# Expert blocks with a split down product, ScalarE evictions and g_ffn applied to the sums

## The chip, the cores and the metric

The kernel runs on 1 core of one Trainium2 chip, as a single launch. The metric is the device time of that core in microseconds (us). Before the change it is 3193.36 us, the median of 3 runs (3192.7 to 3193.63).

## The reference, cut to what matters

The whole is two transformer blocks on 512 tokens of width 1024 in float32. The change is in the expert layer of the first block, and in what follows it at once:

```python
def moe_ffn(h, ...):                      # n = 512 tokens, 64 experts, 8 chosen for each token
    scores = sigmoid(h @ w_router)
    idx = top_k(scores + b_router, 8)
    wts = scores[idx] / sum(scores[idx]) * 2.5
    # each expert works on its own tokens, in blocks of 128 places
    for tok, wt, e in blocks:
        yb = (silu(h[tok] @ w_gate[e]) * (h[tok] @ w_up[e])) @ w_down[e] * wt[:, None]
        routed = routed.at[tok].add(yb)
    return swiglu(h, w_sh_gate, w_sh_up, w_sh_down) + routed

x = x + g_ffn * moe_ffn(h2, ...)          # then a root mean square norm, then the second block
```

An expert has w_gate and w_up of 1024x256 and w_down of 256x1024. On average it has 512 x 8 / 64 = 64 tokens, so of the 128 places of a block about half are empty.

## The kernel before, in words

The engines are TensorE (PE), VectorE (DVE), ScalarE (ACT), GpSimd (POOL) and SyncE (SP). Every engine works through its own list of instructions in the order in which it is written. A scheduling pass of the compiler sets this order ahead of time, for the most part; in a few stretches, such as the end of the last expert, the order of some engines is written out by hand.

Most products are made in float32r, a faster form of float32 that rounds its operands. To keep precision an operand is split (`split`, lines 104 to 106): ScalarE copies it to float32r, the high half `hi` (L105), and VectorE subtracts that from the source, the low half `lo` (L106). `mm` (L102) then makes three passes: hi with hi, hi with lo, lo with hi. The halves of weights are called whi and wlo, 128x1024 each; they come from the pool `pair`, which has three buffers of each name and hands them out in turn. A product that isn't split is made in float32 itself; TensorE then works it off in two pieces.

The expert stage (`moe`) goes through 64 experts and one spare block, 65 blocks, each by `expert_block` (lines 1039 to 1077):
- GpSimd gathers the block's rows of h (`next_rows`, three buffers xg), skipping empty places. TensorE turns them in eight transposes (L1046, p_xt); the result is split into xt, hi and lo.
- The weights come from SyncE's queue as three tiles raw of 1 MB, gate and up in the first two, down in the third; nine such buffers rotate. Gate and up are split in four steps of 1024 columns; each step feeds six products into p_gu (L102), 24 in all.
- ScalarE takes the Silu of the gate part (L1060), VectorE multiplies by the up part (L1061, ea), TensorE turns ea in two transposes (L1064, p_at), VectorE copies the result to eat (L1066).
- The down product (L1072) is float32: eat with the raw weights, four products of 512 columns in eight pieces, into two banks p_y.
- VectorE evicts p_y and multiplies by the routing weight of the place and by the row g_ffn, `grow` (L1075, ey). GpSimd scatters ey and adds it to the rows of a DRAM buffer (L1076). There are two such buffers `yd` and they take turns; empty places go to 128 spare rows below the 512 real ones.

Between the blocks stand other pieces of work: the shared expert (`shared`, `shared_down`), tables of places for the next eight experts (`slots`), the turning of x (`by_tokens`). At the end `routed_first` and `routed_second` read the first buffer yd and add it to the residual rows; a loop for further blocks follows, with no turn when there are none; and `routed` (lines 1200 to 1228) reads the second buffer, adds it, and starts the norm.

Of the kernel before, what the change touches and what calls it, by code (L numbers as in the profile page):

```python
# [10 lines left out]
F32 = mybir.dt.float32  # L11
# [44 lines left out]
class K:  # L56
# [133 lines left out]
    def block1(self):  # L190
        nc, A = self.nc, self.A
        with ExitStack() as es:
# [4 lines left out]

            self.yd = [d.tile([640, 1024], F32, name=f"yd{i}") for i in range(2)]
            self.dr = d = self.pool(es, "b1_dram", space=DRAM)
# [90 lines left out]
    def qkv(self, q, s, w, ctx, mod, hc):  # L290
# [22 lines left out]
        for g in range(7):  # L313
            if g:
                w = self.load_pair(A["w_qkv"][g])
            for j in range(2):
# [25 lines left out]
                elif t < 10:  # L342
                    if t == 8:

                        nc.vector.tensor_copy(self.macc[:, 0:1], d[:, 0:1])
                        nc.vector.memset(self.macc, 0.0)
                        for y in self.yd:
                            for i in range(5):
                                nc.gpsimd.dma_start(y[128 * i:128 * i + 128, :], self.macc)
# [357 lines left out]
    def ffn_begin(self, q):  # L707
# [7 lines left out]
        self.lb = r.tile([128, 64], F32, name="lb")  # L715
        self.r4 = r.tile([128, 4], F32, name="r4")
        r = self.pool(self.rs, "h2r", side="right")
        rows = r.tile([128, 4, 1024], F32, name="h2rows")
# [45 lines left out]
    def moe(self):  # L764
        nc, tc, A = self.nc, self.tc, self.A
        with ExitStack() as es:
# [4 lines left out]
            self.sact = q.tile([128, 2, 512], F32, name="sact")  # L771
            self.grow = q.tile([128, 1024], F32, name="grow")
            self.xr = [t.rearrange("p a b -> p (a b)").rearrange("p (t d) -> p t d", d=1024) for t in self.h2f]
# [265 lines left out]
    def expert_block(self, xg, gi, ws, w, yd):  # L1039
# [20 lines left out]
        nc.scalar.activation(a, pg[:, :256], AF.Silu)  # L1060
        nc.vector.tensor_mul(a, a, pg[:, 256:])  # L1061
        pt = ps.tile([128, 512], F32, name="p_at", tag="tb")
        for k in range(2):
            nc.tensor.transpose(pt[:, 128 * k:128 * k + 128], a[:, 128 * k:128 * k + 128], self.ident)  # L1064
        at = ms.tile([128, 256], F32, name="eat", tag="eat")
        nc.vector.tensor_copy(at, pt[:, :256])  # L1066
        y = ms.tile([128, 1024], F32, name="ey", tag="ey")
        wd = part(2)
        for n in range(2):
            py = ps.tile([128, 512], F32, name="p_y", tag="y")  # L1070
            for k in range(2):
                nc.tensor.matmul(py, at[:, 128 * k:128 * k + 128], wd[:, 1024 * k + 512 * n:1024 * k + 512 * n + 512],  # L1072
                                 start=k == 0, stop=k == 1)
            o = slice(512 * n, 512 * n + 512)
            nc.vector.scalar_tensor_tensor(y[:, o], py, ws, self.grow[:, o], ALU.mult, ALU.mult)  # L1075
        nc.gpsimd.indirect_dma_start(out=yd[:], out_offset=bass.IndirectOffsetOnAxis(ap=gi, axis=0),  # L1076
                                     in_=y[:], in_offset=None, bounds_check=639, oob_is_err=True, compute_op=ALU.add)

# [65 lines left out]
    def routed_second(self):  # L1144
        for x, y in zip(self.xr, self.y0):
            self.nc.vector.tensor_add(x, x, y)

# [52 lines left out]
    def routed(self, q):  # L1200
# [14 lines left out]

        for t in range(4):
            nc.vector.tensor_add(x[t], x[t], ys[t])
            nc.vector.tensor_mul(self.v[:, t, :], x[t], self.gf)
            nc.scalar.activation(junk, x[t], AF.Square, accum_out=s[:, t, 0:1])

            nc.vector.tensor_scalar(s[:, t, 2:3], s[:, t, 0:1], EPS / 1024, EPS * EPS, op0=ALU.mult, op1=ALU.add)
            nc.scalar.activation(junk, self.v[:, t, :], AF.Square, accum_out=s[:, t, 1:2])
            nc.scalar.activation(s[:, t, 3:4], s[:, t, 1:2], AF.Sqrt, bias=s[:, t, 2:3], scale=1.0 / 1024)
            if t:
                scaled(t - 1)
# [1038 lines left out]
```

## Time and profile before

| what | value |
|---|---|
| median of 3 runs | 3193.36 us |
| the profiled execution | 3194.67 us, its span 3192.8 us |
| busy: TensorE, VectorE, ScalarE, GpSimd | 3071.1, 2237.8, 1384.8, 584.6 us |
| expert stage | from about 626 to 1364 us of the span |
| granted TensorE clock, mean | 0.986 |

The span runs from the first to the last instruction; the profiled execution's own time is 1.9 us longer. Busy times are means over stages that have different limits, so the stage that the change touches is read by itself: its windows, what waits in it for what, and the order in time of a few blocks. The end of a matmul in the trace is modelled and products overlap, so the pitch between starts tells what a product takes, not the length shown. A count such as x2 means that rows next to each other were merged. Several instructions of VectorE or ScalarE in a row overlap by a little too.

### The profile page before, as it was taken

How to read it: one execution, taken by the hardware profiler on the slowest of the kernel's cores; microseconds unless marked ns; L12 is line 12 of the kernel's file. 1: busy time of each engine (PE TensorE's matmuls, PEld its weight loads, DVE VectorE, ACT ScalarE, POOL GpSimd, SP SyncE). 2: the span in 40 equal slices, each digit the busy share in tenths (PEclk: the TensorE clock that was granted, in tenths of full speed). 3: DMA queues.
4: the chain of work that ended last, by engine and by line, in shares of the span. 5: the costliest groups of instructions: out<-in, count | busy, mean ns of one | idle time of the engine just before them, and what ended most of it. 6: DMA issues, size and time to landing. Idle time of an engine off the chain costs nothing.

```text
span 3192.8 us, 45059 instructions
## 1 busy us (share of the span) xinstructions
PE 3071.1 (96%) x16976; PEld 2576.9 (81%) x16976; DVE 2237.8 (70%) x4077; ACT 1384.8 (43%) x2195; POOL 584.6 (18%) x452
## 2 busy tenths in 40 slices
PE   7989999999999999969999999999999999999997
PEld 4777888666666766657778788899899999999997
DVE  6567644587777777757633234899998878888885
ACT  5357422454444544434444324444444443333332
POOL 0200000122222222200000000033333322222221
PEclk9999999899999999989999999999999999999999
DMA  7554545399999999952121123387799999999996
GB/s 243 177 155 146 204 172 187 127 356 339 337 342 333 358 354 346 305 172 80 56 72 68 60 93 131 123 295 273 266 329 357 329 333 336 345 344 341 350 342 194
DMA packets 236494, 779.99 MB, mean 244 GB/s; under 512 B 28772, under 2 KB 108132, under 8 KB 190452
## 3 DMA queue, kind: packets, MB, share of 16 engines
q1 hardware_dynamic: 167136, 570.88, 48.7%
q0 software_dynamic: 66368, 200.38, 20.6%
q10 hardware_dynamic: 2772, 5.85, 0.6%
q8 instruction: 134, 2.20, 0.3%
q14 instruction: 84, 0.69, 0.1%
HBM read 692.29 MB, written 101.97 MB: 249 GB/s over the span
## 4 chain that ended last, share of the span: by engine, by line
PE 46%; DVE 5%; issue 4%; ACT 1%; DMA 1%; POOL 0%; POOLq 0%; ACTq 0%; DVEq 0%
PE p_y L102 17%; PE p_pu L102 11%; PE p_za L102 3%; PE p_z L102 2%; PE p_all L1267 1%; PE p_rg L102 1%; PE p_yr L102 1%; PE p_mx L102 1%; DVE wlo L106 1%; DVE prow L2002 1%; PE r_s L1614 1%; PE r_y L1624 1%; PE p_ya L102 1%; PE p_gt L1971 1%; PE p_gt L1972 1%
## 5 line engine op out<-in xcount | busy, mean ns | idle before, releaser
L105 ACT ACTIVATE whi<-raw 128x1024 fp32r<-128x1024 f32 (+1 forms) x686 | 711.4, 1048 | 1115.5 <-PE p_pu L102 261.3
L106 DVE TENSOR_TENSOR wlo<-raw,whi 128x1024 fp32r<-128x1024 f32 (+1 forms) x686 | 822.0, 1206 | 370.4 <-ACT whi L105 361.1
L102 PE MATMUL p_pu<-xp,whi 128*128 128x384 f32 x2048 | 531.9, 338 | 5.0 <-ACT pact L1837 4.8
L102 PEld LDWEIGHTS p_pu<-xp,whi 128*128 128x128 f32 x2048 | 369.4, 188 | 8.0 <-ACT pact L1837 7.6
L102 PE MATMUL p_gu<-whi,xt 128*128 128x512 f32 x1040 | 357.1, 411 | 0.3 <-ACT whi L105 0.2
L102 PE MATMUL p_pu<-xp,wlo 128*128 128x384 f32 x1024 | 344.7, 338 | 4.5 <-DVE wlo L106 4.2
L102 PE MATMUL p_y<-vhi,wlo 128*128 128x384 f32 x1024 | 342.0, 334 | 0.0
L102 PE MATMUL p_y<-vlo,whi 128*128 128x384 f32 x1024 | 342.0, 334 | 0.0
L102 PE MATMUL p_y<-vhi,whi 128*128 128x384 f32 x1024 | 288.8, 334 | 1.4 <-ACT pkept L1837 1.4
L1992 POOL DMA_INDIRECT prow<-in_pu_rows,rows x128 | 197.6, 1544 | 405.4 <-DVE prow L2002 365.4
L1072 PE MATMUL p_y<-raw,eat 128*128 128x512 f32 x520 | 236.2, 595 | 2.7 <-DVE eat L1066 1.5
L102 PEld LDWEIGHTS p_gu<-whi,xt 128*128 128x128 f32 x1040 | 197.6, 191 | 50.6 <-issue 11.0
L102 PE MATMUL p_gu<-wlo,xt 128*128 128x512 f32 x520 | 223.0, 429 | 4.9 <-DVE wlo L106 4.7
L1992 POOL DMA_INDIRECT prow<-in_pv_rows,rows x128 | 140.6, 1099 | 369.3 <-DVE yr L2008 356.1
L102 PEld LDWEIGHTS p_pu<-xp,wlo 128*128 128x128 f32 x1024 | 192.3, 188 | 10.0 <-DVE wlo L106 9.6
L102 PEld LDWEIGHTS p_y<-vlo,whi 128*128 128x128 f32 x1024 | 192.3, 188 | 0.0
L102 PEld LDWEIGHTS p_y<-vhi,wlo 128*128 128x128 f32 x1024 | 192.2, 188 | 0.0
L102 PEld LDWEIGHTS p_y<-vhi,whi 128*128 128x128 f32 x1024 | 187.5, 188 | 1.7 <-ACT pkept L1837 1.7
L1072 PEld LDWEIGHTS p_y<-raw,eat 128*128 128x128 f32 x520 | 97.4, 191 | 101.6 <-issue 89.7
L1076 POOL DMA_INDIRECT yd<-ey,gidx x64 | 117.5, 1836 | 283.7 <-DVE ey L1075 266.5
L2008 DVE SCALAR_TENSOR_TENSOR yr<-prow,pdots,yr 128x1024 f32<-128x1024 f32 x128 | 163.7, 1279 | 0.2
L2002 DVE SCALAR_TENSOR_TENSOR prow<-prow,xr 128x1024 f32<-128x1024 f32 x128 | 155.3, 1216 | 1.8 <-DMA prow<-in_pu_rows,rows 1.7
(704 smaller groups left out, 5550.8 us busy)
## 6 DMA issues: line engine op xcount, KB each, us to landing
raw<-in_w_moe SPq DMA_DIRECT2D x195, 1024.0 KB, 12.2
raw<-in_pu SPq DMA_DIRECT2D x64, 1024.0 KB, 6.6
raw<-in_pv_rows SPq DMA_DIRECT2D x64, 1024.0 KB, 8.1
raw<-in_w_mod SPq DMA_DIRECT2D x24, 1024.0 KB, 6.1
gd<-gst SPq DMA_DIRECT2D x12, 2048.0 KB, 13.5
vgt<-gd SPq DMA_DIRECT2D x32, 768.0 KB, 11.4
actd<-pact SPq DMA_DIRECT2D x54, 384.0 KB, 4.9
vact<-actd SPq DMA_DIRECT2D x54, 384.0 KB, 9.7
```

Source lines behind the costliest of these rows:

```text
L102: nc.tensor.matmul(out, a, b, start=start and i == 0, stop=stop and i == len(passes) - 1)
L105: self.nc.scalar.activation(hi, src, AF.Copy)
L106: (lo_engine or self.nc.vector).tensor_tensor(lo, src, hi.bitcast(F32), ALU.subtract)
L1072: nc.tensor.matmul(py, at[:, 128 * k:128 * k + 128], wd[:, 1024 * k + 512 * n:1024 * k + 512 * n + 512], start=k == 0, stop=k == 1)
L1076: nc.gpsimd.indirect_dma_start(out=yd[:], out_offset=bass.IndirectOffsetOnAxis(ap=gi, axis=0), in_=y[:], in_offset=None, bounds_check=639, ...
L1267: self.nc.tensor.matmul(pts[i][:, :264], w[a][:, 128 * k:128 * k + 128], self.hn[b][:, k, 264 * i:264 * i + 264], start=k == 0 and n == 0, ...
L1614: nc.tensor.matmul(pt[:m, :n], self.rk[r:r + 64, g, 128 * kt:128 * kt + m], self.rq[r:r + 64, g, 512 - n:], start=True, stop=True)
L1624: nc.tensor.matmul(o, sts[kt][:, 128 * (i - kt):128 * (i - kt) + 128], v[:, 128 * kt:128 * kt + 128], start=False, stop=kt == i)
L1971: nc.tensor.matmul(pt[:, i, :], hots["hot2"][:, g, :, t], hots["ghi"][:, g, :, t], start=True, stop=False)
L1992: nc.gpsimd.indirect_dma_start(out=t[:], out_offset=None, in_=A["pu_rows" if i < 128 else "pv_rows"], in_offset=bass.IndirectOffsetOnAxis( ...
L2002: nc.vector.scalar_tensor_tensor(t, t, 1.0, self.xr, ALU.mult, ALU.mult, accum_out=dots[:, k:k + 1])
L2008: nc.vector.scalar_tensor_tensor(self.yr, t, dots[:, k:k + 1], self.yr, ALU.mult, ALU.add)
```

## The change

- **Down product.** The transposed activation is split into eat0 (hi, ScalarE) and eat1 (lo, VectorE). The down weights are split like the others, in two steps of 1024 columns that take buffers from the same pool `pair`, and the product is made in three float32r passes: 12 products of 512 columns in the place of eight float32 pieces. Both banks p_y are open until the second step is done.
- **Weights and eviction.** The routing weight is multiplied in together with the up part (one scalar_tensor_tensor). ScalarE evicts p_y by two plain copies.
- **g_ffn.** `grow` is no longer applied in each block; `routed_second` and `routed` multiply the sums read from yd by it: two products of 128x2048, four of 128x1024, on VectorE. `grow` moves to another pool.
- **Scatter.** An index above 511 is now skipped, so empty places are not written; the buffers yd lose their 128 spare rows, and with them two of the ten DMAs that clear them.

```diff
--- before.py
+++ after.py
@@ -195,7 +195,7 @@
             d = self.pool(self.es, "moe_dram", space=DRAM)
             self.h2d = d.tile([512, 1024], F32, name="h2d")
 
-            self.yd = [d.tile([640, 1024], F32, name=f"yd{i}") for i in range(2)]
+            self.yd = [d.tile([512, 1024], F32, name=f"yd{i}") for i in range(2)]
             self.dr = d = self.pool(es, "b1_dram", space=DRAM)
 
             self.nqd, self.nkd = (d.tile([4, 4, 3, 32, 512], F32, name=n) for n in ("nqd", "nkd"))
@@ -345,7 +345,7 @@
                         nc.vector.tensor_copy(self.macc[:, 0:1], d[:, 0:1])
                         nc.vector.memset(self.macc, 0.0)
                         for y in self.yd:
-                            for i in range(5):
+                            for i in range(4):
                                 nc.gpsimd.dma_start(y[128 * i:128 * i + 128, :], self.macc)
                     d = s.tile([128, 512], F32, name="sp_t", tag="md", bufs=2)
                     nc.vector.tensor_scalar(perm_view(d), src, self.col("b_nk", t - 6), None, op0=ALU.add)
@@ -714,6 +714,7 @@
         self.lgT = r.tile([64, 512], F32, name="lgT")
         self.lb = r.tile([128, 64], F32, name="lb")
         self.r4 = r.tile([128, 4], F32, name="r4")
+        self.grow = r.tile([128, 1024], F32, name="grow")
         r = self.pool(self.rs, "h2r", side="right")
         rows = r.tile([128, 4, 1024], F32, name="h2rows")
         bb = r.tile([128, 1024], F32, name="h2b")
@@ -769,7 +770,6 @@
             for t in self.xg:
                 nc.gpsimd.memset(t, 0.0)
             self.sact = q.tile([128, 2, 512], F32, name="sact")
-            self.grow = q.tile([128, 1024], F32, name="grow")
             self.xr = [t.rearrange("p a b -> p (a b)").rearrange("p (t d) -> p t d", d=1024) for t in self.h2f]
             self.mp = self.pool(es, "mps", 2, space=PSUM)
             self.ms = self.pool(es, "msc", 2)
@@ -1058,23 +1058,25 @@
                             k == 0, k == 7)
         a = ms.tile([128, 256], F32, name="ea", tag="ea")
         nc.scalar.activation(a, pg[:, :256], AF.Silu)
-        nc.vector.tensor_mul(a, a, pg[:, 256:])
+        nc.vector.scalar_tensor_tensor(a, a, ws, pg[:, 256:], ALU.mult, ALU.mult)
         pt = ps.tile([128, 512], F32, name="p_at", tag="tb")
         for k in range(2):
             nc.tensor.transpose(pt[:, 128 * k:128 * k + 128], a[:, 128 * k:128 * k + 128], self.ident)
-        at = ms.tile([128, 256], F32, name="eat", tag="eat")
-        nc.vector.tensor_copy(at, pt[:, :256])
+        at = [ms.tile([128, 256], F32R, name=f"eat{i}", tag=f"eat{i}") for i in range(2)]
+        self.split(*at, pt[:, :256])
         y = ms.tile([128, 1024], F32, name="ey", tag="ey")
         wd = part(2)
+        py = [ps.tile([128, 512], F32, name="p_y", tag="y") for n in range(2)]
+        for k in range(2):
+            hi, lo = (self.pair.tile([128, 1024], F32R, name=n, tag=n) for n in ("whi", "wlo"))
+            self.split(hi, lo, wd[:, 1024 * k:1024 * k + 1024])
+            for n in range(2):
+                self.mm(py[n], tuple(t[:, 128 * k:128 * k + 128] for t in at), (hi[:, 512 * n:512 * n + 512], lo[:, 512 * n:512 * n + 512]),
+                        k == 0, k == 1)
         for n in range(2):
-            py = ps.tile([128, 512], F32, name="p_y", tag="y")
-            for k in range(2):
-                nc.tensor.matmul(py, at[:, 128 * k:128 * k + 128], wd[:, 1024 * k + 512 * n:1024 * k + 512 * n + 512],
-                                 start=k == 0, stop=k == 1)
-            o = slice(512 * n, 512 * n + 512)
-            nc.vector.scalar_tensor_tensor(y[:, o], py, ws, self.grow[:, o], ALU.mult, ALU.mult)
+            nc.scalar.activation(y[:, 512 * n:512 * n + 512], py[n], AF.Copy)
         nc.gpsimd.indirect_dma_start(out=yd[:], out_offset=bass.IndirectOffsetOnAxis(ap=gi, axis=0),
-                                     in_=y[:], in_offset=None, bounds_check=639, oob_is_err=True, compute_op=ALU.add)
+                                     in_=y[:], in_offset=None, bounds_check=511, oob_is_err=False, compute_op=ALU.add)
 
     def spare_places(self):
 
@@ -1143,6 +1145,7 @@
 
     def routed_second(self):
         for x, y in zip(self.xr, self.y0):
+            self.nc.vector.tensor_mul(y, y, self.grow[:, None, :].to_broadcast([128, 2, 1024]))
             self.nc.vector.tensor_add(x, x, y)
 
     def load_after(self, src, x):
@@ -1214,6 +1217,7 @@
             nc.vector.tensor_scalar(self.dg[t], self.ident, s[:, t, 3:4], None, op0=ALU.mult)
 
         for t in range(4):
+            nc.vector.tensor_mul(ys[t], ys[t], self.grow)
             nc.vector.tensor_add(x[t], x[t], ys[t])
             nc.vector.tensor_mul(self.v[:, t, :], x[t], self.gf)
             nc.scalar.activation(junk, x[t], AF.Square, accum_out=s[:, t, 0:1])
```

The scheduling pass sets a new order. Three places show it, each in a quiet stretch of the stage. The names: whi and wlo are halves of weights, xt0 and xt1 the halves of the rows, eat, eat0 and eat1 the activation, raw a tile of weights; a number tells one buffer's use from another's.

TensorE, from the end of a block's gate and up products over the down product, before:

```order
L102 MATMUL p_gu_7464<-whi_7495,xt0_7448 128x512
L102 MATMUL p_gu_7464<-wlo_7496,xt0_7448 128x512
L102 MATMUL p_gu_7464<-whi_7495,xt1_7449 128x512
L1072 MATMUL p_y_7428<-raw_7357,eat_7425 128x512 x2
L1072 MATMUL p_y_7432<-raw_7357,eat_7425 128x512 x2
L102 MATMUL p_gu_7550<-wlo_7552,xt0_7534 128x512
L102 MATMUL p_gu_7550<-whi_7551,xt1_7535 128x512
L102 MATMUL p_gu_7550<-whi_7551,xt0_7534 128x512
```

and now, the second half of a down product and what follows it (whi_7747 is the second step of the next block's gate and up weights):

```order
L102 MATMUL p_y_7684<-whi_7686,eat1_7680 128x512
L102 MATMUL p_y_7685<-whi_7686,eat1_7680 128x512
L102 MATMUL p_y_7684<-whi_7696,eat0_7679 128x512
L102 MATMUL p_y_7684<-wlo_7697,eat0_7679 128x512
L102 MATMUL p_y_7684<-whi_7696,eat1_7680 128x512
L102 MATMUL p_y_7685<-whi_7696,eat0_7679 128x512
L102 MATMUL p_y_7685<-wlo_7697,eat0_7679 128x512
L102 MATMUL p_y_7685<-whi_7696,eat1_7680 128x512
L102 MATMUL p_gu_7736<-whi_7747,xt0_7720 128x512
L102 MATMUL p_gu_7736<-wlo_7748,xt0_7720 128x512
```

Before, the down product stands as four float32 products ahead of the next block's steps and reads no whi or wlo; now it reads two pairs of them, and the next block's second step stands right behind.

VectorE, around the product ea of a block, before:

```order
L106 TENSOR_TENSOR wlo_7466<-raw_7439,whi_7465 128x1024
L106 TENSOR_TENSOR wlo_7476<-raw_7439,whi_7475 128x1024
L106 TENSOR_TENSOR xt1_7535<-p_xt_7536,xt0_7534 128x512
L106 TENSOR_TENSOR xt1_7535<-p_xt_7543,xt0_7534 128x512
L1061 TENSOR_TENSOR ea_7419<-ea_7419,p_gu_7378 128x256
L1075 SCALAR_TENSOR_TENSOR ey_7341<-p_y_7342,wsl_5262,grow_5307 128x512
L106 TENSOR_TENSOR wlo_7486<-raw_7441,whi_7485 128x1024
L1075 SCALAR_TENSOR_TENSOR ey_7341<-p_y_7346,wsl_5262,grow_5307 128x512
L106 TENSOR_TENSOR wlo_7496<-raw_7441,whi_7495 128x1024
```

and now, from the low half of a block's last gate and up step on (wlo_7791 and wlo_7801 are the down weights, wlo_7842 the next block's first step):

```order
L106 TENSOR_TENSOR wlo_7768<-raw_7713,whi_7767 128x1024
L106 TENSOR_TENSOR wlo_7791<-raw_7715,whi_7790 128x1024
L106 TENSOR_TENSOR wlo_7801<-raw_7715,whi_7800 128x1024
L106 TENSOR_TENSOR xt1_7929<-p_xt_7930,xt0_7928 128x512
L106 TENSOR_TENSOR xt1_7929<-p_xt_7937,xt0_7928 128x512
L1061 SCALAR_TENSOR_TENSOR ea_7777<-ea_7777,wsl_5261,p_gu_7736 128x256
L106 TENSOR_TENSOR wlo_7842<-raw_7815,whi_7841 128x1024
L106 TENSOR_TENSOR eat1_7784<-p_at_7780,eat0_7783 128x256
```

Before, two low halves stand ahead of the halves of xt, and the evictions ey between later ones; now three low halves stand in a row ahead of xt and ea, and no eviction is left.

ScalarE, from one Silu (ea) to the next, before:

```order
L1060 ACTIVATE ea_7333<-p_gu_7292 128x256
L105 ACTIVATE whi_7399<-raw_7355 128x1024
L105 ACTIVATE whi_7409<-raw_7355 128x1024
L105 ACTIVATE whi_7465<-raw_7439 128x1024
L105 ACTIVATE whi_7475<-raw_7439 128x1024
L105 ACTIVATE xt0_7534<-p_xt_7536 128x512
L105 ACTIVATE xt0_7534<-p_xt_7543 128x512
L1060 ACTIVATE ea_7419<-p_gu_7378 128x256
```

and now, from the high half of a block's third step up to its Silu:

```order
L105 ACTIVATE whi_7757<-raw_7713 128x1024
L1077 ACTIVATE ey_7683<-p_y_7684 128x512
L1077 ACTIVATE ey_7683<-p_y_7685 128x512
L105 ACTIVATE whi_7767<-raw_7713 128x1024
L105 ACTIVATE whi_7790<-raw_7715 128x1024
L105 ACTIVATE whi_7800<-raw_7715 128x1024
L105 ACTIVATE xt0_7928<-p_xt_7930 128x512
L105 ACTIVATE xt0_7928<-p_xt_7937 128x512
L1060 ACTIVATE ea_7777<-p_gu_7736 128x256
```

The two evictions ey now stand between the high halves of the third and the fourth step, and the two high halves of the down weights (whi_7790, whi_7800) ahead of xt and the Silu.

## Rows read from the trace of the kernel before

**Rows 1.** The page's first line.

```profile
span 3192.8 us, 45059 instructions
```

**Rows 2.** Windows, the expert stage: length, busy us and count by engine, clock, DMA, GB/s.

```profile
626.00:1364.00 738.00, 726.08 (x3116) 493.32 (x3114) 556.11 (x815) 358.95 (x479) 200.92 (x127) 0.99 0.97 335
```

**Rows 3.** Waits, 700 to 1300 us: who waited for whom; us, times, longest us.

```profile
ACT whi L105 <- PE p_gu L102: 196.9, 95, 9.4
...
ACT whi L105 <- DMA raw<-in_w_moe: 6.2, 3, 4.3
...
PE p_gu L102 <- DVE wlo L106: 4.7, 5, 1.6
```

**Rows 4.** Timeline, TensorE: start, length, engine, line, operation, tiles, shapes, count.

```profile
859.66 1.03 PE L1046 MATMUL p_xt<-ident,xg 128*128 128x128 f32 x8
860.45 0.49 PE L102 MATMUL p_gu<-whi,xt 128*128 128x512 f32 x1
860.77 0.38 PE L1064 MATMUL p_at<-ident,ea 128*128 128x128 f32 x2
860.91 0.48 PE L102 MATMUL p_gu<-wlo,xt 128*128 128x512 f32 x1
861.23 0.62 PE L102 MATMUL p_gu<-whi,xt 128*128 128x512 f32 x2
861.69 0.39 PE L102 MATMUL p_gu<-wlo,xt 128*128 128x512 f32 x1
...
863.78 3.60 PE L1072 MATMUL p_y<-raw,eat 128*128 128x512 f32 x8
866.81 0.79 PE L102 MATMUL p_gu<-wlo,xt 128*128 128x512 f32 x1
867.44 0.62 PE L102 MATMUL p_gu<-whi,xt 128*128 128x512 f32 x2
```

**Rows 5.** Timeline, ScalarE, Silu of neighbouring blocks (wait ahead in brackets).

```profile
884.94 0.39 ACT L1060 ACTIVATE ea<-p_gu 128x256 f32<-128x256 f32 x1
885.21 1.07 ACT L105 ACTIVATE whi<-raw 128x1024 fp32r<-128x1024 f32 x1
...
895.05 0.39 ACT L1060 ACTIVATE ea<-p_gu 128x256 f32<-128x256 f32 x1
```

**Rows 6.** Timeline, all engines, part of one block.

```profile
849.62 0.62 PE L102 MATMUL p_gu<-whi,xt 128*128 128x512 f32 x2
...
850.05 1.06 ACT L105 ACTIVATE whi<-raw 128x1024 fp32r<-128x1024 f32 x1 [0.33 <-PE p_gu L102]
...
857.06 1.09 ACT L105 ACTIVATE xt<-p_xt 128x512 fp32r<-128x512 f32 x2 [4.20 <-PE p_gu L102]
...
857.69 1.29 DVE L106 TENSOR_TENSOR xt<-p_xt,xt 128x512 fp32r<-128x512 f32 x2 [1.70 <-ACT xt L105]
...
858.30 2.96 ACT L105 ACTIVATE whi<-raw 128x1024 fp32r<-128x1024 f32 x3
...
859.40 2.36 DVE L106 TENSOR_TENSOR wlo<-raw,whi 128x1024 fp32r<-128x1024 f32 x2
```

**Rows 7.** Groups by line, ScalarE, 600 to 640 us: busy us, mean ns | idle before.

```profile
L785 ACT ACTIVATE grow<-p_gr 128x512 f32<-128x512 f32 x2 | 1.2, 597 | 12.5 <-PE p_gr L738 12.5
```

**Rows 8.** Chain of waits (first row), then VectorE's timeline, end of the stage.

```profile
1370.12 10.29 DMA yd<-ey,gidx
...
1371.80 2.28 DVE L1146 TENSOR_TENSOR h2f<-h2f,raw 128x2048 f32<-128x2048 f32 x1
1381.67 0.24 DVE L1302 MEMSET ckz<- 128x96 f32 x2 [7.59 <-issue]
...
1386.36 1.23 DVE L1218 TENSOR_TENSOR x<-h2f,gf 128x1024 f32<-128x1024 f32 x1
```

**Rows 9.** Windows of 10 us in an early stage, columns as in the second group.

```profile
20.00:30.00 10.00, 7.41 (x30) 1.85 (x29) 7.09 (x9) 6.61 (x9) 0.00 (x0) 1.00 1.00 383
...
190.00:200.00 10.00, 8.19 (x32) 6.45 (x33) 5.45 (x12) 3.99 (x10) 0.00 (x0) 0.66 0.71 179
```

## Prediction

> **What bounds the kernel now.** I read the page first: span 3192.8 us [rows 1], the profiled execution 3194.67 us (1.9 us around the span; the median of the runs shown, 3193.36, lies 1.3 us lower, so sums made on this execution hold for it). Then the windows of the expert stage, which the change rewrites: in the 738 us from 626 to 1364, TensorE is busy 726 us at a clock of 0.99 and the DMA share is 0.97 [rows 2]. Then the waits in it. A long DMA share alone would suggest a transfer bound, but ScalarE waits for weights only 6.2 us in 600, and TensorE waits 4.7 us for a low half. What does wait is ScalarE, 196.9 us in 95 times, for TensorE to release a buffer of the halves [rows 3]. So TensorE bounds the stage, and the splits of weights run just in time behind it.
>
> The timeline gives the pitch. Two float32r products of 512 columns take 0.46 us (861.23 to 861.69), 0.23 each; from 863.78 to 867.44 there are 8 float32 pieces and one float32r, so (3.66 - 0.23) / 8 = 0.43 a piece; eight transposes and one float32r take 1.11 us (859.66 to 860.77), 0.11 a transpose, and the two of p_at about the same [rows 4]. A block is 24 x 0.231 + 8 x 0.428 + 10 x 0.11 = 10.07 us, and two quiet neighbours indeed lie 10.11 us apart, from one Silu to the next [rows 5]. There are 65 blocks (64 experts and one spare). 65 x 10.1 = 657 us; the other 81 us of the stage are the shared expert, the tables of places, the turning of x, start and end.
>
> **What is added and taken away, engine by engine.** TensorE: 8 float32 pieces (3.42 us) become 12 float32r products (12 x 0.231 = 2.77 us), 0.65 us less a block. ScalarE gains two 128x1024 halves at a pitch of 0.95 (three take 2.96), two evictions and one 128x256 copy. No row shows ScalarE evicting p_y; the nearest, the same shape from PSUM to SBUF, takes 0.597 us [rows 7], bounded by the 0.54 us pitch that float32r copies of that shape keep (two in 1.09) [rows 6]; I take 0.50 back to back and 0.60 alone. The 128x256 steps keep 0.27 there (884.94 to 885.21) [rows 5]. ScalarE then works 6 x 0.95 + 2 x 0.50 + 2 x 0.27 + 2 x 0.50 = 8.2 us a block. VectorE gains two 128x1024 differences (two take 2.36, a pitch of 1.15) and loses two products with g_ffn: 6 x 1.15 + 2 x 0.61 + 2 x 0.34 = 8.8 us (0.34 is my estimate for 128x256: half of the 0.61 and a little for its start). By these sums alone TensorE, with 9.4, would still be last. That is not the answer, because the halves share three buffers of each kind and each engine works in its written order.
>
> **The buffers.** Name the halves of a block g0 to g3 (gate and up) and d0, d1 (down, new). With three buffers A, B, C they now lie fixed: g0 A, g1 B, g2 C, g3 A, d0 B, d1 C. Before, the 3.42 us of down products needed no split, and in that time ScalarE and VectorE refilled the buffers. Now the down products hold B and C themselves, and TensorE does the next block's g1 right behind them: the high half of g1 may start only when the sixth down product releases B, that of g2 when the twelfth releases C.
>
> **The loop that results**, on the order of the changed kernel, with these steps: a product releases its buffer 0.43 us after it starts (849.62 to 850.05); a high half is 1.06 long; the next engine starts about 0.05 after a result (xt: 857.06 plus 0.60 to 857.69) [rows 6].
> - VectorE, from the start of g3's low half: three low halves in a row (g3, d0, d1) 3 x 1.15; the two halves of xt 2 x 0.61; the product ea 0.34; g0's low half, to its end, 1.21: 6.22 us, and 0.05 to TensorE.
> - TensorE, from g0's second product: 4 more of g0, then 12 down products; the last starts 16 x 0.231 = 3.70 later and releases C after 0.43.
> - ScalarE: the high half of g2 0.95, the two evictions 1.00 (they stand ahead of g3 in its order), the high half of g3 1.06, 0.05 to VectorE: 3.06. That starts g3's low half of the next block.
> Sum 6.27 + 4.13 + 3.06 = 13.46 us, against 10.1. TensorE's own work in it is 36 x 0.231 + 10 x 0.11 = 9.4, so it would stand still some 4 us a block: ahead of the transposes for xt, which wait for the two xt splits behind g3; ahead of g0; 0.95 us at g1's low half (released 0.43 after the sixth down product, plus 1.06, 0.05, 1.21, 0.05 is 2.80 us, and TensorE wants it after 7 x 0.231 = 1.62; some of this is repaid in the loop); and at g3's low half.
>
> A page of the Trainium skill prices this otherwise: TensorE: Matmul & The Clock Gate, section Back-to-back issue gap, gives about 216 ns for 512 columns. The trace has 0.231 for float32r [rows 4]; by the page the 16 pitches of the loop would be an estimated 0.25 us shorter, 16 us in 65 blocks, and the measured pitch is used.
>
> **The stage.** 65 x 13.46 = 875 us. Of the 81 us of other work part falls into TensorE's pauses (the shared expert's products), part lengthens the loop, since the tables of places are VectorE's work and the turning of x ScalarE's. From both sides: none to all of it, 0 to 81; I take 65, nearer to all, because most of it stands between links of the loop. 940 us against the 737 or so of now: +203.
>
> **The rest.** Transfers: scatters carry only occupied places, so fewer rows; since the stage becomes longer and weights already came in time [rows 3], nothing is won there. The queues of SyncE and GpSimd issue the same DMAs; the weight buffer of the down part is now released by VectorE's split, not by the product, and it has three blocks of slack. At the end the last scatter lands 10.29 us after its issue, and VectorE stands idle 7.59 us for it; the two new products with g_ffn on the first sums are 2.28 us each (as the addition of that shape), 4.6 us, inside that idle time. The four on the second sums are not hidden: 4 x 1.23 = 4.9 us on the path to the norm [rows 8]. The shorter scatter gives something back: none, or at most the 7.59 - 4.6 = 3.0 us after which VectorE is the last one. Net +1.9 to +4.9; I take +3. The cleared rows of the buffers, two small DMAs in a busy early stretch: nothing.
>
> Sum: 3194.67 + 203 + 3 = 3400 us.
>
> **Rivals.**
> 1. TensorE stays the bound (faster). If ScalarE and VectorE ran far enough ahead, the block would be 9.4 us: 65 x 0.65 = 42 us less, 3156 us with the end. For it: the sums 8.2 and 8.8 lie below 9.4, and waits for splits are small now [rows 3]. Against: B and C can't be refilled before the down products end, whatever order one writes. It decides if the loop is under 9.4, 4 us below my sum. 9%.
> 2. The loop holds, but is shorter or swallows all other work. With the whole 81 us in the pauses, 3194.67 + 138 + 3 = 3335; with a loop of 12.7 us as well, 3286. For it: TensorE's pauses are long. Against: each link is a measured duration. 15%.
> 3. The clock falls. In the loop TensorE does only ten transposes and one product in the 3.9 us between g3 and the rest of g0. In the trace the granted clock was 0.66 in a stretch that followed such scattered work, but 1.00 in another with TensorE busy 7.41 of 10 us [rows 9]. At 1.2 GHz the 16 pitches of the loop double, 3.7 us: in every fourth block 60 us (3460), in all 240 (3640). The Trainium skill, TensorE: Matmul & The Clock Gate, section HAM oscillation, describes such a loop that goes cold in each pass because of a wait; by it the second figure. Some falls yes, all no: 20%.
> 4. Gains and losses cancel (within 0.2%, 6 us, about what a measurement of this kernel can tell from no change): 1%.
>
> **Numbers.** Forecast 55%, its own range 3360 to 3440 (other work 25 to 81, plus or minus 0.3 us a block). With the rivals: 3300 leaves out rival 1, rival 4 and a part of 2; 3490 leaves out the worse part of 3. Faster 0.10, same 0.02, slower 0.88.
>
> **What would show it.** The stage then ends near 1565, not 1364, with TensorE busy three quarters of it. Two quiet blocks lie 13 to 14 us apart, from one Silu to the next. TensorE waits for VectorE (xt, wlo) and ScalarE (whi); ScalarE's whi waits for TensorE's p_y. VectorE's idle time falls little. The end is longer by the four products. I am wrong if quiet blocks lie under 11 us apart, or if whi of g1 and g2 starts before the down products end; rival 3 shows as a granted clock under 0.95 in the stage.

## The result and the profile after

The changed kernel takes 3313.62 us (median of 4 runs, 3308.47 to 3316.2); the kernel before took 3193.03 us in runs on the same chip. The ratio is 1.0379, 95% interval 1.0363 to 1.0396: slower, as forecast, by 120 us and not by 207. The time lies inside the range (3300 to 3490) and outside the forecast's own range (3360 to 3440).

The page's first line, which answers to [rows 1]: 116.7 us more span.

```profile
span 3309.5 us, 46137 instructions
```

The window of the expert stage, columns as in [rows 2]: length, busy time and count of each engine, clock, DMA share, GB/s.

```profile
626.00:1482.00 856.00, 728.01 (x3338) 530.67 (x3337) 628.53 (x806) 572.71 (x799) 172.52 (x126) 0.99 0.80 273
```

The stage ends 118 us later. TensorE is busy for 85% of it, not 98%, the DMA share falls from 0.97 to 0.80, and the clock stays at 0.99. The waits in the stretch of [rows 3], 700 to 1300 us, say whom the engines now wait for (us, times, longest):

```profile
DVE wlo L106 <- ACT whi L105: 128.0, 115, 9.4
ACT whi L105 <- PE p_gu L102: 94.1, 97, 5.4
...
PE p_xt L1046 <- DVE xt L106: 55.4, 37, 1.6
...
ACT whi L105 <- PE p_y L102: 24.5, 35, 8.8
```

VectorE waits for ScalarE, ScalarE for TensorE (now for p_y too), TensorE for VectorE: a ring, in which no engine is always busy. Two neighbouring Silu in ScalarE's timeline, which answer to [rows 5]:

```profile
921.91 0.39 ACT L1060 ACTIVATE ea<-p_gu 128x256 f32<-128x256 f32 x1
...
934.07 0.39 ACT L1060 ACTIVATE ea<-p_gu 128x256 f32<-128x256 f32 x1
```

12.16 us; blocks with no other work beside them (quiet blocks) mostly lie 12.13 to 12.17 apart (10.11 before, 13.46 forecast). Over all blocks of the stage the mean is 13.2 (11.2 before). One turn of the ring in the timeline of all engines (start, length, engine, line, what, wait ahead):

```profile
930.58 3.50 DVE L106 TENSOR_TENSOR wlo<-raw,whi 128x1024 fp32r<-128x1024 f32 x3 [0.69 <-ACT whi L105]
...
933.99 1.28 DVE L106 TENSOR_TENSOR xt<-p_xt,xt 128x512 fp32r<-128x512 f32 x2
...
934.73 0.66 PE L1046 MATMUL p_xt<-ident,xg 128*128 128x128 f32 x4 [1.44 <-DVE xt L106]
935.18 0.47 DVE L1061 SCALAR_TENSOR_TENSOR ea<-ea,wsl,p_gu 128x256 f32<-128x256 f32 x1
...
935.57 1.22 DVE L106 TENSOR_TENSOR wlo<-raw,whi 128x1024 fp32r<-128x1024 f32 x1
...
936.85 0.51 PE L102 MATMUL p_gu<-wlo,xt 128*128 128x512 f32 x1 [0.24 <-DVE wlo L106]
...
937.88 0.40 PE L102 MATMUL p_gu<-whi,xt 128*128 128x512 f32 x1
938.12 0.40 PE L102 MATMUL p_y<-whi,eat 128*128 128x512 f32 x1
938.32 1.06 ACT L105 ACTIVATE whi<-raw 128x1024 fp32r<-128x1024 f32 x1 [1.29 <-PE p_gu L102]
...
939.05 0.85 PE L102 MATMUL p_y<-whi,eat 128*128 128x512 f32 x3
...
939.71 1.06 ACT L105 ACTIVATE whi<-raw 128x1024 fp32r<-128x1024 f32 x1 [0.33 <-PE p_y L102]
...
940.68 1.07 ACT L1077 ACTIVATE ey<-p_y 128x512 f32<-128x512 f32 x2
940.68 0.39 PE L102 MATMUL p_y<-whi,eat 128*128 128x512 f32 x1
...
941.63 2.00 ACT L105 ACTIVATE whi<-raw 128x1024 fp32r<-128x1024 f32 x2
...
942.72 1.23 DVE L106 TENSOR_TENSOR wlo<-raw,whi 128x1024 fp32r<-128x1024 f32 x1 [0.69 <-ACT whi L105]
```

Read it against the forecast loop, in its names (g0 to g3 the four gate and up steps, d0 and d1 the two down steps). VectorE: from g3's low half at 930.58 to the start of the product that waits for g0's low half at 936.85 it is 6.27 us; forecast 6.27. ScalarE: from g2's high half at 939.71 over the two evictions and g3's high half to 942.72 it is 3.01; forecast 3.06. TensorE: 936.85 to 939.71 is 2.86; forecast 4.13. The sum is 12.14, the spacing. What differs is the product that releases g2's buffer. The down products begin at 938.12; the sixth starts at about 938.12 + 5 x 0.231 = 939.28, and 0.43 later g2's high half starts. It does not wait for the twelfth. And g1's high half starts at 938.32, 0.44 after the last product of g0 and long before the sixth.

The first and the last Silu of the stage, in the kernel before and then in the changed one:

```profile
637.38 0.39 ACT L1060 ACTIVATE ea<-p_gu 128x256 f32<-128x256 f32 x1
...
1355.56 0.38 ACT L1060 ACTIVATE ea<-p_gu 128x256 f32<-128x256 f32 x1 [6.76 <-PE p_gu L102]
```

```profile
630.17 0.38 ACT L1060 ACTIVATE ea<-p_gu 128x256 f32<-128x256 f32 x1
...
1477.21 0.38 ACT L1060 ACTIVATE ea<-p_gu 128x256 f32<-128x256 f32 x1 [3.33 <-PE p_gu L102]
```

They show where the 116.7 us are: the first comes at 630.17 us (637.38 before), 7.2 less; from the first to the last are 64 intervals, 847.0 us (718.2 before), 128.9 more; from the last Silu to the end of the span 1832.3 us (1837.2 before), 4.9 less.

### The profile page after: what moved, and what is told of

Read it like the earlier page. It is cut to its first block, busy times and chain, and to the rows that moved or that the text cites. A ratio compares the mean times of both kernels' runs of the same rounds, so it can differ in the third digit from the quotient of the medians.

```text
span 3309.5 us, 46137 instructions
## 1 busy us (share of the span) xinstructions
PE 3077.4 (93%) x17236; PEld 2618.5 (79%) x17236; DVE 2322.4 (70%) x4083; ACT 1601.2 (48%) x2520; POOL 555.6 (17%) x450
## 4 chain that ended last, share of the span: by engine, by line
PE 69%; DVE 12%; issue 9%; ACT 5%; DMA 3%; POOL 1%; SPq 0%; POOLq 0%; ACTq 0%; DVEq 0%
PE p_y L102 19%; PE p_pu L102 11%; PE p_gu L102 5%; DVE wlo L106 5%; PE p_za L102 3%; ACT whi L105 3%; PE p_ga L102 3%; PE p_z L102 2%; PE p_all L1271 1%; PE p_in L102 1%; PE p_rg L102 1%; PE p_out L102 1%; PE p_mx L102 1%; PE p_ua L102 1%; PE p_yr L102 1%
## 5 line engine op out<-in xcount | busy, mean ns | idle before, releaser
L105 ACT ACTIVATE whi<-raw 128x1024 fp32r<-128x1024 f32 (+1 forms) x816 | 849.3, 1050 | 1025.5 <-PE p_pu L102 261.5
L106 DVE TENSOR_TENSOR wlo<-raw,whi 128x1024 fp32r<-128x1024 f32 (+1 forms) x816 | 978.1, 1210 | 456.2 <-ACT whi L105 445.0
L102 PEld LDWEIGHTS p_pu<-xp,wlo 128*128 128x128 f32 x1024 | 192.3, 188 | 10.4 <-DVE wlo L106 10.1
L102 PE MATMUL p_y<-whi,eat 128*128 128x512 f32 x520 | 179.2, 406 | 6.2 <-ACT eat L105 6.0
L1078 POOL DMA_INDIRECT yd<-ey,gidx x64 | 104.3, 1630 | 347.0 <-ACT ey L1077 319.2
L1046 PE MATMUL p_xt<-ident,xg 128*128 128x128 f32 x520 | 81.3, 283 | 78.4 <-DVE xt L106 76.9
```

The source lines that it names most:

```text
L102: nc.tensor.matmul(out, a, b, start=start and i == 0, stop=stop and i == len(passes) - 1)
L105: self.nc.scalar.activation(hi, src, AF.Copy)
L106: (lo_engine or self.nc.vector).tensor_tensor(lo, src, hi.bitcast(F32), ALU.subtract)
L1046: nc.tensor.transpose(pt[:, 128 * k:128 * k + 128], xg[:, 512 * g + 128 * k:512 * g + 128 * k + 128], self.ident)
```

## The experiments

Theory L: the block lasts as long as a loop through the three shared buffers. Each ratio is to runs of the kernel before in the same batch (medians 3189 to 3191 us).

**The split down product alone**, in the kernel before; VectorE still evicts and multiplies with `grow`:

```diff
-        at = ms.tile([128, 256], F32, name="eat", tag="eat")
-        nc.vector.tensor_copy(at, pt[:, :256])
+        at = [ms.tile([128, 256], F32R, ...) for i in range(2)]
+        self.split(*at, pt[:, :256])
...
+        py = [ps.tile([128, 512], F32, name="p_y", tag="y") for n in range(2)]
+        for k in range(2):
+            hi, lo = (self.pair.tile(...) for n in ("whi", "wlo"))
+            self.split(hi, lo, wd[:, 1024 * k:1024 * k + 1024])
+            for n in range(2):
+                self.mm(py[n], ...)
...
```

> The kernel before with the down product alone changed: eat and the down weights split, three float32r passes; VectorE still evicts with the weight and g_ffn, scatter as before. Theory L (the down halves share the three buffers with the gate and up halves, and this closes a loop through TensorE, ScalarE and VectorE): still slow, quiet blocks 12.3 to 12.7 us apart (ScalarE's 0.95 us of evictions leave the loop, VectorE's two of 0.66 us enter it), 3310 to 3340 us. Rival V (ScalarE's evictions, which stand between its high halves, are what slows the blocks): about 9.5 to 10.2 us a block, 3150 to 3195 us. Rival W (the split work itself is too much for ScalarE and VectorE): slow too, with VectorE busy nearly all the time.

3370.89 us, ratio 1.0578 (1.0560 to 1.0595); quiet blocks 13.91 us. It is slower than the whole change by some 60 us, so beside a split product evictions on VectorE cost more than those on ScalarE. Not all of this is theirs: in this kernel TensorE's order also has four down products ahead of the rest of g0, which the later runs show to cost something. V falls, and W too, since VectorE is busy 451 of the 600 us from 700 to 1300. L named the sign; its size was 30 us short. The timeline (as above) shows the link that was not counted:

```profile
951.51 0.75 DVE L1078 SCALAR_TENSOR_TENSOR ey<-p_y,wsl,grow 128x512 f32<-128x512 f32 x1 [3.16 <-PE p_y L102]
...
952.18 1.22 DVE L106 TENSOR_TENSOR wlo<-raw,whi 128x1024 fp32r<-128x1024 f32 x1
953.31 0.74 DVE L1078 SCALAR_TENSOR_TENSOR ey<-p_y,wsl,grow 128x512 f32<-128x512 f32 x1
...
953.45 0.50 PE L102 MATMUL p_gu<-wlo,xt 128*128 128x512 f32 x1 [1.05 <-DVE wlo L106]
```

VectorE's eviction waits 3.16 us for p_y, with g1's low half queued behind it, and TensorE waits 1.05 us for that half.

**Everything but the split down product:**

```diff
-        at = [ms.tile([128, 256], F32R, ...) for i in range(2)]
-        self.split(*at, pt[:, :256])
+        at = ms.tile([128, 256], F32, name="eat", tag="eat")
+        nc.vector.tensor_copy(at, pt[:, :256])
...
+            for k in range(2):
+                nc.tensor.matmul(py, at[:, ...], wd[:, ...], start=k == 0, stop=k == 1)
```

> The changed kernel with the float32 down product put back; all else of the change stays (weight folded in, ScalarE evicts, g_ffn on the sums, scatter without empty places). Theory L: quiet blocks 10.1 us apart as before, the end some 5 us shorter, 3180 to 3192 us. Rival V: blocks of 11 us or more, 3250 us or more. Rival W: as theory L.

3196.34 us, ratio 1.0026 (1.0014 to 1.0038); quiet blocks 10.11 us. V falls. L's quiet blocks came; its time, 3180 to 3192, was missed by 4 us. So the split down product carries nearly all of the loss, and beside a float32 product the evictions, the folded weight, g_ffn on the sums and the scatter together cost about 7 us and gain none. From the last Silu to the end this kernel has 2.1 us more than before, against +3 forecast.

**The scatter alone**, in the kernel before:

```diff
-            self.yd = [d.tile([640, 1024], F32, name=f"yd{i}") for i in range(2)]
+            self.yd = [d.tile([512, 1024], F32, name=f"yd{i}") for i in range(2)]
...
-                            for i in range(5):
+                            for i in range(4):
...
-                                     ... bounds_check=639, oob_is_err=True, ...
+                                     ... bounds_check=511, oob_is_err=False, ...
```

> The kernel before with the scatter alone changed: empty places are skipped, the buffers have 512 rows. Theory: the last two scatters, which come one after the other, take about 6 us each and not 10, so the end is 8 us shorter: about 3185 us; blocks 10.1 us apart as before. Rival (the transfers are hidden anyway, the end waits for something else): 3193 us, no change.

3191.01 us, ratio 1.0012 (1.0000 to 1.0023): no gain. The rows of GpSimd and SyncE at the end of its stage:

```profile
1361.39 2.82 POOL L1076 DMA_INDIRECT yd<-ey,gidx  x1 [8.21 <-issue]
1363.19 0.35 SPq L1152 DMA_DIRECT2D raw<-in_w_z  x1
1372.60 0.81 SPq L1210 DMA_DIRECT2D yx<-yd  x2
```

The same rows before:

```profile
1370.12 2.84 POOL L1076 DMA_INDIRECT yd<-ey,gidx  x1 [8.54 <-issue]
1371.96 0.35 SPq L1152 DMA_DIRECT2D raw<-in_w_z  x1
1381.21 1.84 SPq L1210 DMA_DIRECT2D yx<-yd  x4
```

From the last scatter's issue to the read of its buffer are 11.2 us (11.1 before), although only occupied places are written: a load of 1 MB (in_w_z) is issued 1.8 us behind the scatter's start and runs beside it. In the changed kernel it is issued earlier, and the same stretch takes 7.3 us:

```profile
1474.61 0.34 SPq L1155 DMA_DIRECT2D raw<-in_w_z  x1
1485.89 2.05 POOL L1078 DMA_INDIRECT yd<-ey,gidx  x1 [13.43 <-ACTq L1097]
1493.20 0.81 SPq L1213 DMA_DIRECT2D yx<-yd  x2
```

That the load is the cause was read from such rows, not tried. The other traces fit it in the main. In the eight kernels that skip empty places and issue the load ahead of the scatter, the stretch takes 7.0 to 9.0 us; in the split alone, which writes all 128 places and also issues the load ahead, it takes 8.9. With the load behind the scatter it takes 9.0 (own buffers, 0.3 us behind), 11.1 and 11.2 (the two above, 1.8 behind) and 13.6 (high products first with own buffers, 6.6 behind). So the number of places written makes little difference here.

**Two own buffers for the down halves**, and seven weight tiles, not nine, to make room:

```diff
-RAW2 = 6
+RAW2 = 4
+            self.dpair = self.pool(es, "dpair", 2)
-            hi, lo = (self.pair.tile(...) for n in ("whi", "wlo"))
+            hi, lo = (self.dpair.tile(...) for n in ("dhi", "dlo"))
```

> The changed kernel with two buffers of their own for the two down halves (hi and lo, 16 KB of a partition), paid for by two of the nine 1 MB weight buffers (seven remain). Theory L: the loop is cut, TensorE bounds the blocks again, quiet blocks 9.5 to 10.3 us apart, 3130 to 3190 us. Rival W: engine loads are unchanged, so 12.1 us a block and 3300 to 3315 us.

3225.07 us, ratio 1.0114 (1.0097 to 1.0131). About 85 of the 120 us come back (1.0379 - 1.0114 of 3190) with no product, split or eviction taken away, so the waits for the three shared buffers are most of the cause and W falls. The run has five buffers of each half in all, not three, so it doesn't tell sharing from scarcity; five shared ones were not tried. The mean from Silu to Silu is 11.8 us (13.2 in the changed kernel, 11.2 before), the blocks are uneven (6.7 to 21.9; before, 5.6 to 23.4), and TensorE still waits for wlo, xt and eat: L's number, 3130 to 3190, was too good.

**High products first in the down steps:**

```diff
-            for n in range(2):
-                self.mm(py[n], ...)
+            x = [t[:, 128 * k:128 * k + 128] for t in at]
+            for w, t, f, l in ((hi, x[0], True, False), (hi, x[1], False, False), (lo, x[0], False, True)):
+                for n in range(2):
+                    nc.tensor.matmul(py[n], t, w[:, 512 * n:512 * n + 512], start=k == 0 and f, stop=k == 1 and l)
```

> The changed kernel with one thing altered: in each step of the down product the four products that read the high half come first and the two that read the low half last. So the sixth down product no longer holds the high half; in the order of this kernel it is the second product after g0 that releases it, and the fourth one before the end of the second step that releases the other. No product is added or taken away. Theory L (a block lasts as long as the loop through the three shared buffers): the release comes 4 pitches of 0.231 us = 0.92 us sooner, and the two evictions no longer stand between the high halves of g2 and g3; the loop then goes through VectorE's low halves of g1, g2, g3 and is 11.0 to 11.3 us instead of 12.14. 65 x about 1.05 = 68 us less: 3230 to 3265 us. Rival S (the sums of work on the three engines and the just-in-time splits set the block, the moment of release doesn't matter): 3305 to 3320.

3307.07 us, ratio 1.0361 (1.0344 to 1.0378): about 6 us less by the ratios (1.0379 - 1.0361 of 3190), which is not clear of noise, since the two intervals overlap; L said 50 to 84. The theory as I priced it failed here. Quiet blocks are 12.31 us, and the timeline shows a second loop:

```profile
932.48 1.06 ACT L105 ACTIVATE whi<-raw 128x1024 fp32r<-128x1024 f32 x1 [0.33 <-PE p_gu L102]
...
937.62 0.73 PE L1076 MATMUL p_y<-whi,eat 128*128 128x512 f32 x2 [0.47 <-ACT eat L105]
...
938.18 0.39 PE L102 MATMUL p_gu<-wlo,xt 128*128 128x512 f32 x1
...
939.55 2.96 ACT L105 ACTIVATE whi<-raw 128x1024 fp32r<-128x1024 f32 x3 [1.98 <-PE p_gu L102]
...
944.79 1.06 ACT L105 ACTIVATE whi<-raw 128x1024 fp32r<-128x1024 f32 x1 [0.33 <-PE p_gu L102]
```

Its links: the last product of g0 releases the buffer of g1 (939.55); g1's halves, then 11 products of g1 and g2; the last of them releases d1's buffer (932.48 in the turn shown, 944.79 in the next); d1's halves, xt, ea, the transposes, eat, and two down products that now stand ahead of the rest of g0 (937.62). 944.79 - 932.48 = 12.31. If the first loop is shorter now, it is hidden behind this one, which I had left out.

**High products first in all steps**, gate and up too:

```diff
-                for kk in range(2):
...
-                    self.mm(pg, ...)
+                k0 = 4 * i + 2 * j
+                for w, h in ((hi, 0), (hi, 1), (lo, 0)):
+                    for kk in range(2):
+                        nc.tensor.matmul(pg, xt[h][:, k0 + kk, :], w[:, 512 * kk:512 * kk + 512], ...)
```

> As the run before, and the gate and up steps too make their four high products first and the two low ones last. Each high half is released two products sooner, each low half is wanted three products later, and the order that results puts the transposes for xt earlier, so that VectorE makes xt ahead of the low halves. Theory L: 10.3 to 10.9 us a block, 3200 to 3240 us. Rival S: no different from the changed kernel, 3305 to 3320.

3241.56 us, ratio 1.0161 (1.0144 to 1.0178), quiet blocks 11.27 us. About 70 us less than the changed kernel (1.0379 - 1.0161 of 3190) with the same work and the same three buffers: the order of the work, and with it when a buffer comes free and when its contents are wanted, is what costs. S falls; L's range (3200 to 3240) is missed by 2 us.

**The same with two own buffers:**

```diff
-RAW2 = 6
+RAW2 = 4
+            self.dpair = self.pool(es, "dpair", 2)
-            hi, lo = (self.pair.tile(...) for n in ("whi", "wlo"))
+            hi, lo = (self.dpair.tile(...) for n in ("dhi", "dlo"))
```

> As the run before, and the down halves have two buffers of their own (dhi, dlo); the third kind of weight tile has seven buffers instead of nine to make room. Theory L: no down product stands between a release and a high half of gate or up any more, so TensorE's own work of 9.4 us a block is the last bound: blocks of 9.4 to 10.0 us, 3155 to 3195 us. Rival S: the splits stay just in time, 11 us or more a block, 3225 us or more as with own buffers alone.

3221.97 us, ratio 1.0095 (1.0078 to 1.0112). L missed by 27 us and S's 3225 or more by 3, so S is nearer, and the order, worth 70 us with three buffers, is worth next to nothing with five. The blocks are uneven as with own buffers alone (mean 11.65, other work included). In 700 to 1350 us TensorE is busy 604 of 650 us. What orders these blocks was not taken apart further; no version here beats the kernel before.

**Seven weight tiles alone**, the control:

```diff
-RAW2 = 6
+RAW2 = 4
```

> The changed kernel with seven weight tiles raw instead of nine and nothing else: the control for the two runs with own buffers. Theory L: weights came early enough, 3308 to 3320 us. Rival R (the tiles held back the transfers, and that is what own buffers alone had left to lose): 3330 us or more, with ScalarE's whi waiting for the DMA.

3316.94 us, ratio 1.0392 (1.0375 to 1.0409): as the changed kernel. R falls. The blocks are slower here than with own buffers, so this alone does not clear the transfers there; but between 700 and 1300 us no engine waits for a weight transfer with own buffers alone, and ScalarE waits 2.0 us for one with high products first and own buffers.

**A third eviction:**

```diff
-        for n in range(2):
+        for n in (0, 1, 0):
             nc.scalar.activation(y[:, 512 * n:512 * n + 512], py[n], AF.Copy)
```

> The changed kernel, in which ScalarE evicts the first bank p_y a second time, to the same place: one more 128x512 copy a block, which stands between the high half of g3 and that of d0; the rest of the order is as it was. ScalarE's sum rises from 8.2 to 8.7 us of a block of 12.1. Theory L (a block lasts as long as its loop): the high half of d0 comes 0.5 us later behind that of g3, VectorE had 0.2 to spare there (1.15 against 0.95), so the loop is 0.3 to 0.4 longer: quiet blocks 12.4 to 12.6 us, 3330 to 3345 us. Rival S (sums of work): ScalarE has 4 us of idle time a block, 3308 to 3320 us.

3343.66 us, ratio 1.0485 (1.0464 to 1.0505): 30 us more, in L's range, though ScalarE has idle time in every block. Quiet blocks are 12.85, above L's 12.4 to 12.6. From the start of g3's low half to xt it is now 3.71 us (3.41 before the edit), the 0.3 that the extra copy was to cost; the other 0.4 comes from TensorE's order, which did not stay as it was: four down products now stand ahead of the rest of g0. So the time fits L, but not all of it is the copy's.

**The low half of d1 on GpSimd:**

```diff
-            self.split(hi, lo, wd[:, 1024 * k:1024 * k + 1024])
+            self.split(hi, lo, wd[:, 1024 * k:1024 * k + 1024], nc.gpsimd if k else None)
```

> The changed kernel with one instruction a block given to another engine: the low half of d1 is subtracted by GpSimd, not VectorE. Nobody wants it before the end of the down product. The orders of ScalarE and VectorE are as they were without it; on TensorE four of the down products move ahead of the rest of g0. Theory L: one link of 1.15 us leaves VectorE's part of the loop, and xt is then bound by ScalarE: 0.4 to 1.0 us less a block, 11.1 to 11.8 us, 3250 to 3290 us. Rival S: VectorE's sum was 8.8 of 12.1 us and was no bound, so 3308 to 3320 us. Rival G (GpSimd takes over 4 us for it, or slows VectorE): 3325 us or more.

3339.98 us, ratio 1.0462 (1.0445 to 1.0480), quiet blocks 12.48. L missed: VectorE's stretch from g3's low half to xt shrinks only from 3.41 to 3.14 us, because xt then waits for ScalarE, which waits for g2's last product to release d1's buffer, the second loop again; and TensorE has the order of the run before, which costs 0.6 here (12.48 = 12.14 - 0.27 + 0.61). G's time came, but not for its reason: GpSimd takes 2.36 us for the half and nobody waits for it in the quiet blocks.

**That, with high products first in all steps:** the two edits together, the second being

```diff
+            self.split(hi, lo, wd[:, 1024 * k:1024 * k + 1024], nc.gpsimd if k else None)
```

> The kernel with high products first in all steps (3241.56 us, quiet blocks 11.27 us), and the low half of d1 on GpSimd as in the run before. Theory L: VectorE's low halves and xt are in the loop of that kernel too, up to 1.15 us less a block: 10.1 to 10.9 us, 3170 to 3225 us, which may pass the kernel before. Rival S: 3235 to 3248 us. Rival G: 3250 us or more.

3469.97 us, ratio 1.0872 (1.0852 to 1.0892). G holds, by more than it said. The timeline:

```profile
933.36 2.94 POOL L106 TENSOR_TENSOR wlo<-raw,whi 128x1024 fp32r<-128x1024 f32 x1
...
933.93 3.46 DVE L106 TENSOR_TENSOR wlo<-raw,whi 128x1024 fp32r<-128x1024 f32 x1 [1.63 <-ACT whi L105]
...
937.45 1.22 PE L1058 MATMUL p_gu<-wlo,xt 128*128 128x512 f32 x2 [2.29 <-DVE wlo L106]
```

A low half of VectorE that falls beside GpSimd's takes 3.46 us where it takes 1.22 alone, and TensorE waits 2.29 us for it here and 83.3 us in 37 waits from 700 to 1300 us. The window 700 to 1300 us, columns as above, shows what follows:

```profile
700.00:1300.00 600.00, 486.31 (x1992) 360.42 (x1992) 407.25 (x447) 341.91 (x481) 197.44 (x114) 0.87 0.71 235
```

The clock is 0.87: the third rival of the prediction, in another kernel. It is a mean of two levels: windows of 4 us behind such a wait show down to 0.50, the level of 1.2 GHz.

## Why the prediction came out as it did

- **What bounds the kernel before.** Right: with the float32 down product back and all other edits in, quiet blocks are 10.11 us and the time is 3196 us.
- **The loop, and so the sign.** Right that the down halves turn a stage bound by TensorE into a loop through shared buffers: own buffers win back about 85 of 120 us, and another order of the same products about 70.
- **The step that failed** is "with three buffers A, B, C they now lie fixed", and from it "that of g2 when the twelfth releases C". The buffers do not go round in the written order of the program. In the trace g1's high half waits only for g0's last product, so of the three buffers it takes g0's, and g2's waits for the sixth down product. How the built program allots them is inferred from these waits. The term "TensorE 4.13" measured 2.86; the other two terms, 6.27 and 3.06, measured 6.27 and 3.01. 65 x (13.46 - 12.14) = 86 us, which is nearly the whole miss of 3400 - 3313.6. The sentence "B and C can't be refilled before the down products end, whatever order one writes" falls with it. The prediction had named the sign that would refute it: whi of g1 and g2 starting before the down products end. They do (938.32 and 939.71; the last down product starts at 940.68), and g2 is the one that counts, since the loop itself had priced g1 ahead of that end. That 3313.6 us still lies in the stated range is owed to the share kept for rival 2, a shorter loop, and not to the loop as priced, whose own range began at 3360.
- **Other work.** 65 us of the 81 were to stay: 856 - 65 x 12.14 = 67. The number came by luck. Between the first and the last Silu nothing was swallowed: 718.2 - 64 x 10.11 = 71.2 us of other work before, 847.0 - 64 x 12.14 = 70.0 now. What is missing lies at the two edges of the windows: the first Silu stood 11.4 us behind the window's start and stands 4.2 behind it now, and from the last one to its end are 4.8 us, not 8.4.
- **A slip.** "0.95 us at g1's low half" does not follow from its own numbers: 2.80 - 1.62 is 1.18. Nothing in the sum hangs on it.
- **The end.** +3 forecast, -4.9 measured. The four products with g_ffn do cost what was said (the norm begins with one of 1.22 us ahead of each sum). Two things were missed: the last scatter is issued 8.7 us after the last Silu, not 14.6, and it is read 7.3 us after its issue, not 11.1; 5.9 and 3.8 us less and 4.9 more make -4.8. Before, the last scatter stood 10.1 us behind the one ahead of it (issued at 1360.03) and most likely waited for that to land; with longer blocks it stands 15.1 behind (1470.84). The cap of "at most 3.0 us" for a shorter scatter held its start fixed. The scatter edit alone does not shorten this stretch.
- **The start.** The first Silu comes 7.2 us earlier, but most likely not by the change. In the 13 traces of this case it comes anywhere from 628.38 us (the split alone, whose edit touches nothing ahead of the stage) to 637.38 (the kernel before, the latest of all). Against the split alone, the kernel before is 8.4 us late already at the step ahead of the routing scores (ScalarE's `r`, 607.59 against 599.17 us). So these 7.2 us are better read as spread between executions.
- **Rivals.** TensorE as the bound (3156) did not come; it is busy 85%. A shorter loop came, but not with the other work swallowed. The clock did not fall (0.99), though TensorE stalls 1.44 us ahead of the transposes in each quiet block; in the last run, with stalls of 2.29 us and more, it is 0.87. The loop that goes cold in each pass in the Trainium skill, TensorE: Matmul & The Clock Gate, section HAM oscillation, waits there for a transfer, and longer than TensorE does here, so it does not speak for this loop as it came out.

## What to carry to other kernels

Before an operand is split further, count who holds each buffer of the halves and until which instruction: a pool that just served one stream turns into a ring of waits when a second one shares it, and an engine's idle share then says nothing on what bounds the block. Price such a loop from the trace link by link, but take the buffers from the built program and not from the order of the source, and look for a second loop nearly as long, since cutting one link then wins almost nothing (about 6 us of 50 to 84 here, within noise) while stretching one still costs (30 us for one more copy, with the order that it brought).

## What the runs showed of the hardware

- VectorE's subtraction from SBUF to SBUF waits for one of GpSimd's that runs beside it: a half that takes 1.22 us alone takes 3.46 beside GpSimd's 2.94, and ends 1.1 us after it; beside 37 of the 57 halves that GpSimd makes from 640 to 1540 us in the last run, VectorE's takes 3.42 to 3.48. Beside the subtraction from PSUM (xt, 1.29 us for two) there was no such loss. The Trainium skill, SBUF — State Buffer, section SBUF: two separate sides, describes an exclusive lock of a shared port, which VectorE takes for an instruction with two SBUF inputs; both observations fit it. It does not say why GpSimd's own half takes 2.94 us there and 2.36 in the run before.
- With only the occupied places written, the last scatter was read no sooner beside a 1 MB load issued 1.8 us behind it (11.2 us after its issue, against 11.1 with all 128 places). With the load ahead of it the time was 7.0 to 9.0 us, and 8.9 with all places written.
